# Packing the queries on GpSimd, with the loads, weights and bias rows around it laid out anew, in a hybrid decoder layer

## The chip, the cores and the metric

The kernel runs on one core of a Trainium2 chip. Its engines are TensorE (PE in the profile, with the weight loads as PEld), VectorE (DVE), ScalarE (ACT), GpSimd (POOL) and SyncE (SP). SP only issues transfers, ACT issues some too; an issue of ACT is shown as ACTq, one of SP as SPq. The metric is the device time of one execution in microseconds. Chances of "same" mean within 0.2% of the time before.

## The reference

The layer takes x (2048 tokens of 1024 channels, float32) and computes two mixers beside each other, an output projection and a squared-ReLU MLP:

```
n = RMSNorm(x)
gq, gk, gv, gr, glow, dq, dk, dv = split(n @ W_in)
o_a = GLA(gq, gk, gv, log_sigmoid(glow @ w2 + b) / 16)      # 4 heads, chunks of 64
o_a = RMSNorm per head(o_a) * g * silu(gr)
o_b = dilated attention(dq, dk, dv, rel_bias)                # 8 heads of 64
h = x + [o_a ; o_b] @ W_out
h = h + relu(RMSNorm(h) @ W_ff1)^2 @ W_ff2
y = RMSNorm(h)
```

GLA is linear attention with a forget gate, computed in chunks with a state of 64x128 per head that is carried from chunk to chunk. The dilated attention has three branches, with (window, dilation) of (128, 1), (512, 4) and (2048, 16). In a branch with dilation d the tokens are taken with stride d, and each query of a block of 128 sees the keys of its own block and the one before it, up to 128 steps back; a bias is added by bucket of distance. The three outputs are summed with weights proportional to their softmax denominators.

## The kernel before

All products are made in float32 or in a rounded format of it (fp32r). For the large ones each operand is split in two parts, high and low, and `mm3` (lines 66 to 69) sums three matmuls into a PSUM bank: high by high, low by high, high by low. The large products are done in seven block products in place of eight, so most stages run over seven jobs j in the order 1, 2, 5, 6, 3, 4, 7 and add or subtract blocks in between.

There are four stages. Up to about 589 us the **projections** run: 18 groups (nine groups of W_in's columns for two halves of the tokens), each of seven jobs, 126 jobs in all. `load_w` (line 181) loads pieces of the weights on SP's queue. `prep` (187) splits the weights of a job, on ACT (line 197) and DVE (199, 201), into one of three buffers `combs` (176), two jobs ahead of the product; on POOL it also forms the block sums that the next jobs need. `product` (270) multiplies. Six groups are narrow (two times 128 columns: the queries and keys of both mixers); there the weights are held in the array and 512 tokens are moved, so that the result is transposed. Three are wide (two times 256, or 264); there the tokens are held and the weights moved. A buffer of `combs` is laid out for pieces of 264 columns in any case, so the pieces of 128 or 256 columns stand 1,056 bytes apart. `finish` (230) stores the results in DRAM, for most groups on ACT's queue.

During the second half, `bias_rows` (320) makes for each branch and head a row of 384 biases and stores it (`rowD`), and `spread_bias` (333) copies each row 128 times within DRAM (`rbD`), so that a later load can read it with each partition shifted by one. It is called three times, six jobs apart, once for each branch; each is one transfer of 1,536 KB on SP's queue.

Next is the **mixer** (about 589 to 993 us). The dilated attention is cut into 160 units, 20 for each of eight heads: 4 for the branch with dilation 16 (`br` 2), and 8 each for `br` 1 and `br` 0. A unit computes scores on PE (lines 624, 626), adds the bias and takes the row minimum on DVE (636), exponentiates on ACT (637), transposes on PE (646), copies the transposed probabilities out of PSUM on ACT or DVE in turn (653, 655), multiplies with the values on PE (665) and copies the result on DVE (668). Step k of the main loop interleaves the scores of unit k+3, the transposes of unit k and the values of unit k-2.

For the branches 2 and 1 the queries of a block are not neighbours. `pack_q` (567) copies a head's queries into a buffer `qp` where they are, in four parts of 128x512 for each of the two branches, so 64 copies in all, on ACT (line 578). The main loop calls them four to one units ahead of the branch's first unit. `load_head` (518) loads a head's queries (`qs`, each half of the partitions in its own transfer) and its keys in two parts (`k1`, `k2`, each twice): six transfers of 512 KB, thirteen units ahead. After two heads `combine` (684) loads stored results of two branches, computes the weights on DVE (699 to 710) and sums on POOL (716, 718), for the last two heads on DVE.

The GLA part, called the gated part here, runs in the same loop: `gla_steps` (798) is a generator of 79 short steps, five for each block of 128 tokens. It has PE products, exponentials and squares on ACT (784, 785, 818, 820), products on POOL (786, 787, 833, 834) and the state's update on DVE (844, 847). The loop takes a step of it from unit G0 on, GE times in 100 units: with 16 and 65, the steps end near unit 138.

At the start of the mixer, the loads are written in this order (862 to 867): the first head's queries and keys, the values of the three branches, the biases of the three branches (eight loads each; POOL reorders those of branches 1 and 0, lines 559 and 562), then the gated part's buffers, constants and first blocks.

Last come the **output projection** (to about 1228 us) and the **MLP**, which the change doesn't touch.

What sets the order of the work: only the first part of the projections has its order written out by hand. Elsewhere a planner goes through the program with estimated durations and puts, on each engine and each queue, the operation next that is ready and stands first in the program; an operation written later can so come earlier. An engine or a queue then runs in the order planned, and waits where its next operation isn't ready. Large tiles share 25 slots of 8,448 bytes in each partition, so a load also waits until a slot is free.

Of the kernel before, what the change touches and what calls it, by code (L numbers as in the profile page):

```python
# [10 lines left out]
F32 = mybir.dt.float32  # L11
FR = mybir.dt.float32r
I32 = mybir.dt.int32
AF = mybir.ActivationFunctionType
# [19 lines left out]
XSC = {0: (3,), 1: (4,), 2: (5,), 3: (), 4: (6,)}  # L34
TOP = (5,)
OTHER = [7, 9, 10, 11, 12] + [14 * k + n for k in (1, 2, 3) for n in (0, 4, 7, 8, 9)]
G0, GE = 16, 65
RELOAD = (10, 11, 12)
BANKS = {"a": 2, "c": 3, "d": 2, "o": 1}

# [1 line left out]
def emit(tc, a, stop=99):  # L42
# [15 lines left out]
    def view(t, shape):  # L58
        n = int(np.prod(shape))
        names = "abcd"[:len(shape)]  # L60
        return t[:, :n].rearrange(f"p ({' '.join(names)}) -> p {' '.join(names)}", **dict(zip(names, shape)))
# [111 lines left out]
    jobs = [(g, j) for g in range(2 * NG) for j in order]  # L173
    w_in = a["w_in"].rearrange("o (c p) n -> p (o c) n", p=128)
    raws = [view(slot("wraw"), (2, 4, 264)) for _ in range(2)]
    combs = [view(slot("wcomb", FR), (2, 4, 264)) for _ in range(3)]
    TF = {j: [slot(f"tb{j}", FR) for _ in range(2)] for j in order}
    TB = {j: [view(t, (4, 512)) for t in TF[j]] for j in order}
    nTD = dram.tile([7, 128, 4, 512], F32, name="nTD")
# [1 line left out]
    def load_w(g, n, k):  # L181

        if g < 2 * NG:
            _, c0, w = groups[g % NG]
            SP.dma_start(raws[n][:, k, :, :w], w_in[:, 4 * k:4 * k + 4, c0 + n * w:c0 + n * w + w])

    def prep(at):

        if at >= len(jobs):
            return  # L190
        g, j = jobs[at]
        kind, _, w = groups[g % NG]
        (a11, a12), (a21, a22) = [[raws[n][:, k, :, :w] for k in range(2)] for n in range(2)]
        hi, lo = combs[at % 3][:, 0, :, :w], combs[at % 3][:, 1, :, :w]
        src = {1: a11, 2: a12, 5: a21, 6: a21, 3: a12, 4: a22, 7: a21}[j]
        sc = scales.get(kind, 1.0)
        A.activation(hi, src, AF.Copy, scale=sc)  # L197
        if sc == 1.0:
            V.tensor_tensor(lo, src, hi.bitcast(F32), op=OP.subtract)  # L199
        else:  # L200
            V.scalar_tensor_tensor(lo, src, sc, hi.bitcast(F32), op0=OP.mult, op1=OP.subtract)
        if j == 2:
            G.tensor_tensor(a21, a21, a22, op=OP.add)
        if j == 5:
            G.tensor_tensor(a21, a21, a11, op=OP.subtract)
            load_w(g + 1, 0, 0)
            G.tensor_tensor(a12, a12, a21, op=OP.subtract)
        if j == 6:
            G.tensor_tensor(a21, a22, a21, op=OP.subtract)
        if j == 3:  # L210
            load_w(g + 1, 0, 1)
        if j == 4:
            load_w(g + 1, 1, 1)
        if j == 7:
            load_w(g + 1, 1, 0)
# [54 lines left out]
    def product(at, i):  # L270

        g, j = jobs[at]
        kind, _, w = groups[g % NG]
        p = ps("acao"[banks[0] % 4])
        banks[0] += 1
        B, W = TB[j], [combs[at % 3][:, q, :, :w] for q in range(2)]
        n = w
        if w == 128:
            n = 512
            for c in range(4):  # L280
                mm3(p, W[0][:, c], W[1][:, c], B[0][:, c], B[1][:, c], c == 0, c == 3)
        else:
            p = p[:, :w]
            tk = slice(i * 128, i * 128 + 128)
            for c in range(4):
                mm3(p, B[0][:, c, tk], B[1][:, c, tk], W[0][:, c], W[1][:, c], c == 0, c == 3)

        def rest():
            X, c11, c12, c21, c22 = [v[:, i * n:i * n + n] for v in (CX, *C[0], *C[1])]
            q = p  # L290
            if kind == "dq":
                q, ix, i11, i12, i21, i22 = [v.rearrange(f"p (c {o}) -> p c r i", c=4, i=8) for v, o in
                                             ((p, "r i"), *((v, "i r") for v in (X, c11, c12, c21, c22)))]
            else:
                ix, i11, i12, i21, i22 = X, c11, c12, c21, c22
            if j == 1:
                A.activation(ix, q, AF.Copy)  # L297
            elif j == 2:
                V.tensor_tensor(i11, q, ix, op=OP.add)
                finish(g, 0, 0, i)  # L300
            elif j == 5:
                A.activation(i22, q, AF.Copy)
            elif j == 6:
                V.tensor_tensor(ix, q, ix, op=OP.add)
                G.tensor_tensor(c12, X, c22, op=OP.add)
            elif j == 3:
                V.tensor_tensor(i12, q, i12, op=OP.add)
                finish(g, 0, 1, i)
            elif j == 4:
                A.activation(i21, q, AF.Copy)  # L310
            else:
                V.tensor_tensor(ix, q, ix, op=OP.add)
                G.tensor_tensor(c21, c21, X, op=OP.add)
                V.tensor_tensor(c22, c22, X, op=OP.add)
                finish(g, 1, 0, i)
                finish(g, 1, 1, i)

        return rest
# [11 lines left out]
            V.tensor_copy(rbo[:, d], p[:8, :384])  # L330
        SP.dma_start(rowD, rbo)

    def spread_bias(d):

        row = rowD[:, d]
        SP.dma_start(rbD[d].rearrange("h p n -> p h n"),
                     bass.AP(tensor=row.tensor, offset=row.offset, ap=[[0, 128], [3 * 384, 8], [1, 384]]))

    def split(hi, lo, src):
        A.activation(hi, src, AF.Copy)  # L340
# [154 lines left out]
    for at in range(5, len(jobs)):  # L495
        g = jobs[at][0]
        if at + 2 > 6:
            prep(at + 2)
        if at in (7 * NG - 9, 7 * NG - 8):
            back.append(reload(order[at - 7 * NG + 9]))  # L500
        for i in range(4 if groups[g % NG][2] > 128 else 1):
            product(at, i)()
        if g == NG - 1:
            back.pop(0)()
            if at + 2 < 7 * NG:
                back.append(reload(order[at + 2 - 7 * NG + 7]))
        if at in OTHER:
            next(other)
        if at == 7 * NG + 2:
            bias_rows()  # L510
        if at in (7 * NG + 8, 7 * NG + 14, 7 * NG + 20):
            spread_bias((at - 7 * NG - 8) // 6)
    if stop <= 1:
        es.close()
        return
# [2 lines left out]
    def load_head(h):  # L518
        pr, hh = divmod(h, 2)
        qs, k1, k2 = slot("qs", FR, S), slot("k1", FR, S), slot("k2", FR, S)  # L520
        rows = slice(64 * hh, 64 * hh + 64)
        for dup in range(2):
            half = slice(64 * dup, 64 * dup + 64)
            SP.dma_start(qs[half].bitcast(F32), qD[pr][dup, rows])
            SP.dma_start(k1[half].bitcast(F32), kD[pr][0, rows])
            SP.dma_start(k2[half].bitcast(F32), kD[pr][1, rows])
        return qs, k1, k2

    def load_v(pr, br):
# [37 lines left out]
    def pack_q(h, br, part):  # L567
# [7 lines left out]
        else:  # L575
            dst = dst.rearrange("e (r i) -> e r i", r=16)[:, 4 * part:4 * part + 4]
            src = src.rearrange("e (i r) -> e r i", r=16)[:, 4 * part:4 * part + 4]
        A.activation(dst, src.bitcast(F32), AF.Copy)

    def windows(br, n):  # L580

# [279 lines left out]

    pairs, outs = {0: load_head(0)}, {}
    ring["pes"], ring["pts"] = view(slot("pe"), (4, 512)), view(slot("pt"), (4, 512))
    vs = {(0, br): load_v(0, br) for br in (2, 1, 0)}
    for d in (2, 1, 0):
        load_bias(d)
    gla_start()
    WOAT = {(7, 2): 3, (7, 1): 2, (6, 0): 2, (7, 0): 1}

    def alternate(*streams):  # L870
# [229 lines left out]
    for at, t in enumerate(tiles):  # L1100
# [3 lines left out]
        h = u[:, 1]  # L1104
# [258 lines left out]
```

## Time and profile before

| | us |
|---|---|
| median of 3 runs | 2445.02 (2440.99 to 2446.39) |
| the profiled execution | 2445.35 |
| its span, first to last instruction | 2443.6 |
| PE busy, of the span | 2331.5 |
| DVE, ACT, POOL busy | 1585.7, 1196.0, 488.6 |
| mean granted clock of PE | 0.982 |

A line of the profile's groups or of the timeline names the line of the program, the engine and the operation, then the tile written, an arrow, and the tiles read, with the shape. In a timeline the first two numbers are the start and the duration in us; several operations of one kind in a row are merged, as x6; in brackets stand the idle time of the engine before and what ended it. Matmuls overlap in the pipeline: one shows 0.39 us, but the next starts about 0.23 us later, so steps are read from the starts. The granted clock is 1.00 most of the time and 0.50 in some stretches of 3.4 or 6.8 us, mostly after PE was idle.

### The profile page before, as it was taken

The page shows a single profiled execution, that of the slowest core. Times are in us where ns is not written, and L with a number is a line of the kernel's source. Part 1 is how long each engine was busy: PE and PEld are TensorE (multiplying, and loading weights), DVE is VectorE, ACT ScalarE, POOL GpSimd, SP SyncE. Part 2 cuts the span into 40 slices and gives each one's busy share as a digit, 9 for nine tenths or more (in the row PEclk, how much of TensorE's full clock was granted, in tenths as well). Part 3 has the DMA queues.
Part 4 walks back from the last instruction along what each step waited for, and adds up shares of the span by engine and source line. Part 5 has one row for each costly group of instructions (what it writes and reads, how often), then busy time and mean ns, then how long its engine had stood idle before and what let it go on. Part 6 is the DMA issues. An engine that isn't in the chain of part 4 may idle for free.

```text
span 2443.6 us, 34989 instructions
## 1 busy us (share of the span) xinstructions
PE 2331.5 (95%) x12648; PEld 1998.8 (82%) x12648; DVE 1585.7 (65%) x2971; ACT 1196.0 (49%) x2215; POOL 488.6 (20%) x425
## 2 busy tenths in 40 slices
PE   6999997999889989999999999999999999999998
PEld 6877887778889888888878887888888888888887
DVE  6877666764567768644677778877774354555554
ACT  5565434534767768323455556655553232234323
POOL 5555435444044534000000000000000000001002
PEclk8999998999999989999999999999999999999999
DMA  6457763747677875567754446644458576556653
GB/s 156 122 157 233 231 197 99 213 147 198 161 186 213 208 197 172 172 215 233 254 195 158 142 147 207 213 168 145 143 194 289 167 276 210 185 189 231 224 165 103
DMA packets 343514, 459.16 MB, mean 188 GB/s; under 512 B 19572, under 2 KB 216453, under 8 KB 337070
## 3 DMA queue, kind: packets, MB, share of 16 engines
q1 hardware_dynamic: 317854, 418.92, 55.8%
q10 hardware_dynamic: 25488, 38.02, 4.4%
q8 instruction: 99, 1.62, 0.3%
q14 instruction: 73, 0.60, 0.1%
HBM read 294.03 MB, written 167.55 MB: 189 GB/s over the span
## 4 chain that ended last, share of the span: by engine, by line
PE 74%; DMA 8%; DVE 7%; ACT 5%; issue 3%; POOL 2%; ACTq 0%; SPq 0%; POOLq 0%; DVEq 0%
PE ps_a L67 8%; PE ps_a L69 8%; PE ps_a L68 8%; PE ps_c L67 7%; PE ps_c L69 7%; PE ps_c L68 7%; PE ps_d L67 4%; PE ps_d L69 4%; PE ps_d L68 4%; PE ps_a L665 3%; PE ps_o L67 3%; PE ps_o L69 3%; PE ps_o L68 3%; PE ps_d L646 2%; DMA wraw<-w_in 2%
## 5 line engine op out<-in xcount | busy, mean ns | idle before, releaser
L1197 POOL TENSOR_TENSOR suma<-suma,gs 128x512 f32<-128x512 f32 x16 | 23.3, 1472 | 1153.2 <-ACT scr L1195 1153.1
L341 DVE TENSOR_TENSOR ca<-ra,ca 128x1024 fp32r<-128x1024 f32 x112 | 137.8, 1230 | 163.1 <-ACT ca L340 163.1
L340 ACT ACTIVATE ca<-ra 128x1024 fp32r<-128x1024 f32 x112 | 118.0, 1053 | 224.9 <-PE ps_c L69 184.5
L340 ACT ACTIVATE w1comb<-w1raw 128x512 fp32r<-128x512 f32 x224 | 139.5, 627 | 159.6 <-PE ps_c L69 56.6
L665 PE MATMUL ps_a<-v,pt 128*128 128x65 f32 x1200 | 181.1, 263 | 13.0 <-ACT pt L653 10.3
L665 PEld LDWEIGHTS ps_a<-v,pt 128*128 128x128 f32 x1200 | 174.5, 199 | 18.6 <-ACT pt L653 12.0
L341 DVE TENSOR_TENSOR w1comb<-w1raw,w1comb 128x512 fp32r<-128x512 f32 x224 | 153.8, 689 | 53.9 <-ACT w1comb L340 53.6
L637 ACT ACTIVATE pe<-pe,O 128x256 f32<-128x256 f32 (+1 forms) x384 | 155.3, 455 | 59.6 <-DVE O L636 54.9
L646 PE MATMUL ps_d<-ident,pe 128*128 128x128 f32 x600 | 149.6, 285 | 8.6 <-DVE gla L796 6.8
L636 DVE CUSTOM_DVE_ANT_0 pe<-ps_c,nb 128x256 f32<-128x256 f32 (+1 forms) x384 | 126.7, 360 | 45.2 <-PE ps_d L646 25.5
L197 ACT ACTIVATE wcomb<-wraw 128x512 fp32r<-128x512 f32 (+2 forms) x126 | 96.4, 774 | 98.7 <-PE ps_a L69 23.3
L199 DVE TENSOR_TENSOR wcomb<-wraw,wcomb 128x512 fp32r<-128x512 f32 (+2 forms) x84 | 99.3, 1187 | 58.7 <-ACT wcomb L197 56.0
L340 ACT ACTIVATE cb<-rb 128x1024 fp32r<-128x1024 f32 x56 | 59.4, 1060 | 159.2 <-PE ps_o L68 105.8
L67 PE MATMUL ps_c<-hb,w1comb 128*128 128x512 f32 x336 | 131.6, 392 | 4.3 <-ACT hb L340 4.3
L68 PE MATMUL ps_c<-hb,w1comb 128*128 128x512 f32 x336 | 131.5, 391 | 1.6 <-DVE w1comb L341 1.6
L69 PE MATMUL ps_c<-hb,w1comb 128*128 128x512 f32 x336 | 131.1, 390 | 0.0
L67 PE MATMUL ps_c<-cb,ca 128*128 128x512 f32 x336 | 130.7, 389 | 0.0
L68 PE MATMUL ps_c<-cb,ca 128*128 128x512 f32 x336 | 130.7, 389 | 0.0
L69 PE MATMUL ps_c<-cb,ca 128*128 128x512 f32 x336 | 130.7, 389 | 0.0
L67 PE MATMUL ps_a<-wcomb,tb 128*128 128x256 f32 (+1 forms) x336 | 99.1, 295 | 19.2 <-ACT acc L297 12.5
L646 PEld LDWEIGHTS ps_d<-ident,pe 128*128 128x128 f32 x600 | 105.5, 184 | 11.1 <-DVE gla L796 7.3
L1063 ACT ACTIVATE acc<-acc 128x512 f32<-128x512 f32 x128 | 79.7, 631 | 56.3 <-DVE acc L1083 35.8
(352 smaller groups left out, 7247.1 us busy)
## 6 DMA issues: line engine op xcount, KB each, us to landing
ra<-actD SPq DMA_DIRECT2D x56, 1024.0 KB, 6.2
actD<-acc SPq DMA_DIRECT2D x192, 256.0 KB, 2.4
rb<-w_ff SPq DMA_DIRECT2D x72, 512.0 KB, 4.6
w1raw<-w_ff SPq DMA_DIRECT2D x32, 1024.0 KB, 5.6
k<-kD SPq DMA_DIRECT2D x32, 512.0 KB, 10.4
rb<-hTD SPq DMA_DIRECT2D x14, 1024.0 KB, 5.6
wraw<-w_in SPq DMA_DIRECT2D x48, 256.0 KB, 3.5
boD<-O SPq DMA_DIRECT2D x8, 1056.0 KB, 5.5
```

The lines of the kernel that those rows point to most:

```text
L67: T.matmul(out, sh, mh, start=first, stop=False)
L68: T.matmul(out, sl, mh, start=False, stop=False)
L69: T.matmul(out, sh, ml, start=False, stop=last)
L197: A.activation(hi, src, AF.Copy, scale=sc)
L199: V.tensor_tensor(lo, src, hi.bitcast(F32), op=OP.subtract)
L340: A.activation(hi, src, AF.Copy)
L341: V.tensor_tensor(lo, src, hi.bitcast(F32), op=OP.subtract)
L636: V.tensor_tensor_reduce(p, s, bias, scale=1.0, scalar=BIG, op0=OP.add, op1=OP.min, accum_out=nm)
L637: A.activation(p, p, AF.Exp, bias=nm, scale=-1.0)
L646: T.transpose(pb[:, i * 128:i * 128 + 128], src, ident)
L665: T.matmul(self.b.opsum[:, n % 4], self.pt[:, i * 128:i * 128 + 128], self.b.v[:, blk, cols], start=first, stop=last)
L1063: A.activation(v, v, AF.Relu)
```

## The change

There are six edits.

- `pack_q` copies on POOL instead of ACT.
- The gated part starts at unit 8 instead of 16 and takes 56 steps in 100 units instead of 65.
- `load_head` loads both halves of the queries first, then both halves of the first part of the keys, then of the second.
- The weights' buffers of the projections are laid out by the width of the group: pieces of 128 or 256 columns now stand 1,024 bytes apart, those of 264 columns 1,056 bytes as before. A new function `comb` gives the two parts for `prep` and `product`.
- `spread_bias` copies the rows of two heads of one branch at a time, on ACT's queue, so twelve transfers of 384 KB take the place of three of 1,536 KB. They are written three jobs apart, over jobs 72 to 105, from branch 2 to branch 0; before, branch 0 came first.
- At the start of the mixer the loads are written by branch, bias before values, and the gated part's loads come after those of branch 2.

```diff
-G0, GE = 16, 65
+G0, GE = 8, 56
...
-    combs = [view(slot("wcomb", FR), (2, 4, 264)) for _ in range(3)]
+    combs = [slot("wcomb", FR) for _ in range(3)]
...
+    def comb(at, w):
+
+        t = view(combs[at % 3], (2, 4, max(w, 256)))
+        return [t[:, q, :, :w] for q in range(2)]
...
-        hi, lo = combs[at % 3][:, 0, :, :w], combs[at % 3][:, 1, :, :w]
+        hi, lo = comb(at, w)
...
-        B, W = TB[j], [combs[at % 3][:, q, :, :w] for q in range(2)]
+        B, W = TB[j], comb(at, w)
...
-    def spread_bias(d):
+    def spread_bias(d, h):
 
-        row = rowD[:, d]
-        SP.dma_start(rbD[d].rearrange("h p n -> p h n"),
-                     bass.AP(tensor=row.tensor, offset=row.offset, ap=[[0, 128], [3 * 384, 8], [1, 384]]))
+        row = rowD[h:, d]
+        A.dma_start(rbD[d][h:h + 2].rearrange("h p n -> p h n"),
+                    bass.AP(tensor=row.tensor, offset=row.offset, ap=[[0, 128], [3 * 384, 2], [1, 384]]))
...
-        if at in (7 * NG + 8, 7 * NG + 14, 7 * NG + 20):
-            spread_bias((at - 7 * NG - 8) // 6)
+        if 7 * NG + 8 <= at < 7 * NG + 44 and at % 3 == 0:
+            spread_bias(2 - (at - 7 * NG - 8) // 12, (at - 7 * NG - 8) // 3 % 4 * 2)
...
-        for dup in range(2):
-            half = slice(64 * dup, 64 * dup + 64)
+        halves = [slice(64 * dup, 64 * dup + 64) for dup in range(2)]
+        for dup, half in enumerate(halves):
             SP.dma_start(qs[half].bitcast(F32), qD[pr][dup, rows])
-            SP.dma_start(k1[half].bitcast(F32), kD[pr][0, rows])
-            SP.dma_start(k2[half].bitcast(F32), kD[pr][1, rows])
+        for part, t in enumerate((k1, k2)):
+            for half in halves:
+                SP.dma_start(t[half].bitcast(F32), kD[pr][part, rows])
...
-        A.activation(dst, src.bitcast(F32), AF.Copy)
+        G.tensor_copy(dst, src)
...
-    vs = {(0, br): load_v(0, br) for br in (2, 1, 0)}
+    vs = {}
     for d in (2, 1, 0):
         load_bias(d)
-    gla_start()
+        vs[0, d] = load_v(0, d)
+        if d == 2:
+            gla_start()
```

## The prediction

> **What bounds the kernel now.** I read the page's first part, then the busy time of each engine by stage, then what PE's idle times ended on, and last the timelines of the other engines around those. The page says that PE is the bound:
>
> ```profile
> PE 2331.5 (95%) x12648; PEld 1998.8 (82%) x12648; DVE 1585.7 (65%) x2971; ACT 1196.0 (49%) x2215; POOL 488.6 (20%) x425
> ```
>
> By stage (columns: stretch, length, then PE, PEld, DVE, ACT, POOL busy, granted clock, DMA share, GB/s) PE is never idle in the feed-forward part, which the change doesn't touch, and idle for 12, 15 and 14 us in three stretches of the mixer:
>
> ```profile
> 585.00:640.00 55.00, 43.23 (x340) 41.43 (x340) 28.95 (x131) 40.15 (x77) 13.08 (x20) 0.88 0.84 200
> 640.00:900.00 260.00, 245.41 (x2002) 233.87 (x2001) 178.91 (x744) 188.65 (x488) 101.53 (x107) 0.97 0.78 199
> 900.00:1010.00 110.00, 96.26 (x771) 89.81 (x771) 91.54 (x357) 71.91 (x176) 40.02 (x37) 0.95 0.59 178
> 1540.00:2000.00 460.00, 460.00 (x2032) 380.88 (x2030) 300.99 (x415) 222.66 (x345) 6.04 (x4) 1.00 0.57 194
> ```
>
> So a gain can come from PE's idle times before 1010 us, from the half clock after them, or from a shorter step of PE. The timeline of PE shows the three large idle times in the mixer (in brackets: idle before, and what ended it):
>
> ```profile
> 626.54 2.39 PE L665 MATMUL ps_a<-v,pt 128*128 128x65 f32 x10 [5.54 <-ACT pt L653]
> ...
> 724.32 0.58 PE L624 MATMUL ps_c<-k,qs 128*128 128x256 f32 x1 [6.32 <-DVE O L636]
> ...
> 905.00 1.11 PE L646 MATMUL ps_d<-ident,pe 128*128 128x128 f32 x4 [6.39 <-DVE gla L796]
> ```
>
> The first is ACT's. Its queue holds packs in bursts, and exponentials and copies of probabilities stand behind them:
>
> ```profile
> 617.87 5.86 ACT L578 ACTIVATE qp<-qs 128x512 fp32r<-128x512 f32 x6 [2.31 <-DMA qs<-qD]
> 623.54 0.46 ACT L637 ACTIVATE pe<-pe,O 128x256 f32<-128x256 f32 x1
> 623.91 1.93 ACT L578 ACTIVATE qp<-qs 128x512 fp32r<-128x512 f32 x2
> ```
>
> The second and third are DVE's: it stands in its queue before the combine's first operation, whose loads are late, although ACT has a burst at 715.24 too:
>
> ```profile
> 723.75 0.17 DVE L699 TENSOR_TENSOR small<-O,cmb 128x16 f32<-128x16 f32 x1 [8.27 <-DMA cmb<-boD]
> ...
> 902.09 0.17 DVE L699 TENSOR_TENSOR small<-O,cmb 128x16 f32<-128x16 f32 x1 [8.76 <-DMA cmb<-boD]
> ```
>
> Before the mixer the one large idle time is PE's 11.4 us up to 380.95, ended by ACT's L297. ACT's own timeline shows why it came late: stores of the projections stand in its queue and are let go one by one.
>
> ```profile
> 359.48 0.53 ACTq L266 DMA_DIRECT2D vN<-acc  x1
> 359.75 1.08 ACT L197 ACTIVATE wcomb<-wraw 128x1056 fp32r<-128x1056 f32 x1
> 367.56 0.53 ACTq L266 DMA_DIRECT2D vN<-acc  x1
> 372.24 0.33 ACTq L264 DMA_DIRECT2D vD<-acc  x1
> 373.87 0.53 ACTq L266 DMA_DIRECT2D vN<-acc  x1
> ```
>
> The three transfers that spread the bias rows were issued by SP at 349.79 to 351.2 and land after 17.1 us in the median, and the weight load issued at 354.12 landed 19.7 us later, at 373.85. The stores move on just when these land (their data had been ready since 365.5). So slow transfers on SP's queue held ACT.
>
> Last, PE's steps. In the projections with the weights held, and in the feed-forward products of the same shape:
>
> ```profile
> 519.55 0.39 PE L69 MATMUL ps_c<-tb,wcomb 128*128 128x512 f32 x1
> ...
> 522.12 0.39 PE L69 MATMUL ps_a<-tb,wcomb 128*128 128x512 f32 x1
> ```
>
> ```profile
> 1299.39 0.39 PE L67 MATMUL ps_a<-hb,w1comb 128*128 128x512 f32 x1
> ...
> 1302.11 0.39 PE L67 MATMUL ps_c<-hb,w1comb 128*128 128x512 f32 x1
> ```
>
> These are 11 steps in 2.57 us, 0.2336 each, and 12 in 2.72, 0.2267 each, at a granted clock of 1.00 both times.
>
> **The change part by part.** The sum is made against the profiled execution: 2445.35 us, of which 2443.6 are the span and 1.75 lie around it. The median of the runs shown is 2445.02, so nothing has to be shifted.
>
> *Weights at multiples of 1 KB.* Pieces of the weights stood 1,056 bytes apart; the feed-forward pieces stand 512 bytes apart. If that is the difference, the 1,008 matmuls of 512 columns in the six narrow groups save 0.0069 us each, 7.0 us, in stretches where PE is busy throughout (20.00 of 20 from 540 to 560). The 1,344 of 256 columns step by 0.118 (from 339.77 to 342.01, 19 steps); half of 0.2267 would save up to 6 us more, but the mixer's score products, whose operands stand at multiples of 512 bytes, show 0.12 as well, so I take nothing there. The 672 of 264 columns keep their spacing. Ends: 13 us gained, or nothing, if something else in the projections makes the step long; a loss is left out, because every row at such spacings has the short step. I take -7.
>
> *Bias rows in twelve pieces on ACT's queue.* What can go is the 11.4 us, and about 2.5 us in which PE ran at half clock afterwards (380.95 to about 386): 14 us. What comes are twelve issues on ACT, by SP's rows 0.62 us each, 7.4 us, past exponentials and weight copies. They are written three jobs apart, but the planner issued the three of before back to back, though they are written six jobs apart; so I expect the twelve bunched soon after the row table lands at 349.8. Then ACT loses some 7 us while PE still has products with prepared weights, and the stores wait again, though for transfers a quarter as large and not behind the weight load. Ends: -14 (spread out, all hidden) and +6 (ACT's 7.4 us on PE's path, the old wait kept). I take -7, halfway to the full gain, because the weight load no longer stands behind 4.7 MB in its own queue.
>
> *Start of the mixer.* PE waits 2.39 us for the gated part's loads, 2.08 for the first pack, 1.33 for an exponential, and loses 1.5 at half clock: 7.3 us. The gated loads now come ahead of sixteen bias loads, so the 2.39 should go; ACT begins its exponentials without the eight packs it ran from 593.31 to 601. But the packs are now behind POOL's copies of the bias (0.61 to 0.64 us for 256 columns), which end at 598.97; the first pack at the end of these would set the first score back from 594.4 to about 600. Values and bias loads only swap places on SP: 42 issues to the same end. Ends -7 and +6, and I take 0.
>
> *Packs on POOL.* ACT loses 64 packs of 1.09 us, 70 us in all. On PE's path were 5.54, then 1.30 and 1.07 at 825 and 829, 1.76 at 856, with half clock after the first (2.5 us lost) and after the last (3.4): 15.6 us. POOL gains 64 copies of 512 columns; by the bias copies, 1.25 us each, 80 us, in a stretch where it is busy 155 of 425 us. This is hidden as long as a head's packs are done before its first score. Head 1's queries landed at 617.9 and its packs are needed some 20 us later; eight take 10 us. Behind a pack that waits for its queries stand the gated part's products and the combine's, which PE and DVE wait for in turn. Queries loaded ahead of keys bring their second half forward by two of six loads; the keys' end is the same. Ends: -15.6, and +5 if the gated part is held as the exponentials were. I take -10, about two thirds, because the burst at 618 is alone in being plainly what ended the wait.
>
> *The combine's late loads* (6.32 and 6.39, with 1.5 at half clock after each) are not touched. The planner orders SP anew, so between -16 and +8; I take 0.
>
> *Gated part from unit 8.* Its 79 steps end at unit 150 in place of 138, of 160. That moves seven of them, 1.4 blocks of about 4 us on PE, into the last stretch, where PE had 3.9 us idle between 960 and 1000, but DVE was busy 33 of 40. Ends -4 and +5; I take 0.
>
> Sum: -7 - 7 + 0 - 10 + 0 + 0 = -24, so 2445.35 - 24 = 2421 us.
>
> **The rivals.**
>
> *Packs late on POOL (slower).* POOL works in order, and its operations often wait: L833 up to 21.7 us for ACT, L716 up to 4.7 for DVE. A pack behind such a wait makes PE wait at the first score of a head. One such wait costs what the one at 724 does, 6.3 and 1.5, some 8 us. There are seven changes of head. With the packs' gain lost and -14 from the first two terms, two late heads (16) decide for slower; four give 2445 - 14 + 32 = 2463. For it: that ACT's packs did just this. Against it: 20 us of lead, and POOL idle from 607.5 to 635.4.
>
> *Bias issues bunched on ACT.* +6 in place of -7: 2434.
>
> *Little happens.* The short step isn't due to the spacing, and PE's idle times only move to the next late load: 2445, give or take 5. For it: half of the large idle times are the combine's loads.
>
> *DVE held by POOL.* L847, with both inputs in SBUF, takes 0.42 us in the median but up to 2.31, and 19.9 us in 30 where 12.6 would do: 7.3 us lost, with POOL busy 155 us. With 235 us it would be 11.1, so 3.8 us more of DVE, all on the path at worst: 2425. The Trainium skill (SBUF — State Buffer, section SBUF: two separate sides) has this as a rule: GpSimd and VectorE share a pair of ports, held for a whole instruction, against VectorE operations with two SBUF inputs or in a two-port mode. By that rule the trace agrees in L847, and in the scores' L636 (one input from PSUM, 0.426 us at most), which stays free; the rule speaks against this move, but only for few operations.
>
> **How the numbers follow.** The forecast (2421) gets 0.52, the bunched issues (2434) 0.14, the held DVE (2425) 0.06, little happens 0.08, late packs 0.20. A change below 0.2%, 4.9 us, can't be told from none. Faster: 0.52 + 0.14 + 0.06 = 0.72; same 0.08; slower 0.20. The likeliest case alone spans 2400 to 2442 by its ends (they won't all fall together); the range reaches up into the late packs, to 2454.
>
> **What would show it.** Steps of 0.227 in the narrow projections; no 11 us of PE idle near 370, and where ACT issues the bias rows; no ACT burst at 618 and no PE wait after it; POOL's packs near 1.25 us, and ended before each head's first score. It is wrong if PE's waits end on packs, if L699 still waits 8 us more often than twice, or if the step stays at 0.2336.

## The result and the profile after

The changed kernel takes 2430.9 us in the median of 6 runs (2429.18 to 2433.72), the kernel before 2448.08 (2440.99 to 2452.97) on the same chip: a ratio of 0.9931, with a 95% interval from 0.9913 to 0.9949. That is 0.7% faster, 17.2 us by the medians. The forecast was 2421 us, the range 2400 to 2454. The profiled execution of the changed kernel took 2433.72 us (span 2431.9) against 2445.35 before, 11.6 us less: it is the longest of its six, so the traces show only these 11.6 of the 17.2 us. Most lines of the changed program stand 5, 6 or 8 further down: ACT's weight copy L197 is now L202, the stores' copy L310 is L315, `pack_q`'s copy L578 is L584, and the combine's first operation L699 is L705.

The page's first part, of the changed kernel:

```profile
PE 2327.0 (96%) x12648; PEld 1999.9 (82%) x12648; DVE 1595.3 (66%) x2971; ACT 1142.5 (47%) x2151; POOL 550.3 (23%) x489
```

ACT lost 53 us and POOL gained 62, where the prediction had 70 and 80: the packs have moved. PE still bounds the kernel. The stretches of the mixer and of the MLP, in the columns of before (stretch, length, busy PE, PEld, DVE, ACT, POOL, granted clock, DMA share, GB/s):

```profile
585.00:640.00 55.00, 48.96 (x406) 47.34 (x405) 33.80 (x158) 31.64 (x86) 32.09 (x40) 0.94 0.95 221
640.00:900.00 260.00, 242.20 (x2020) 232.62 (x2019) 187.41 (x778) 158.48 (x450) 146.42 (x153) 0.96 0.79 205
900.00:1010.00 110.00, 97.17 (x720) 89.27 (x720) 90.15 (x316) 58.81 (x146) 38.75 (x34) 0.94 0.50 160
1540.00:2000.00 460.00, 460.00 (x2032) 380.96 (x2031) 298.26 (x404) 219.78 (x336) 6.04 (x4) 1.00 0.58 196
```

In the first stretch PE is busy 5.7 us longer and issues 66 matmuls more: the burst of packs on ACT near 618 is gone. The MLP is as it was. From the starts of PE's instructions, the 11.6 us come from these parts: the projections' last product starts 2.2 us earlier (588.5 to 586.3), the first score comes 1.1 us later after it (6.0 to 7.0), from the first score to the first transpose of the output projection go 13.1 us less (398.9 to 385.8), the output projection takes 4.4 more, the first half of the MLP 1.8 less. The largest idle times of PE in the mixer, in its timeline:

```profile
593.34 0.58 PE L630 MATMUL ps_c<-k,qp 128*128 128x256 f32 x1 [5.52 <-POOL qp L584]
...
707.66 0.77 PE L819 MATMUL ps_o<-gla 128*128 128x256 f32 x1 [5.09 <-DVE gla L853]
...
888.22 0.47 PE L671 MATMUL ps_a<-v,pt 128*128 128x65 f32 x1 [7.91 <-DVE pt L661]
```

The wait of 5.54 us behind ACT's burst has no successor. At the start PE waits for the first pack, on POOL; near 707 for a DVE operation of the gated part; near 888 still for DVE, which stood before the third combine:

```profile
887.39 0.17 DVE L705 TENSOR_TENSOR small<-O,cmb 128x16 f32<-128x16 f32 x1 [9.81 <-DMA cmb<-boD]
```

The start in POOL's timeline: the packs stand behind a copy of the bias that waited for its load, the bound that the prediction had named.

```profile
591.65 0.60 POOL L565 COPY nb<-nb 128x256 f32<-128x256 f32 x1 [3.56 <-DMA nb<-rbD]
592.20 0.14 POOL L538 MEMSET v<- 128x32 f32 x1
592.26 7.95 POOL L584 CAST qp<-qs 128x512 fp32r<-128x512 f32 x8
```

In the projections the twelve transfers of bias rows are in ACT's timeline, eight of them within 6 us, and below them PE's idle times that stand in the place of the 11.39 us up to 380.95:

```profile
351.63 1.92 ACTq L341 DMA_DIRECT2D rbD<-rowD  x3
...
357.05 0.60 ACTq L341 DMA_DIRECT2D rbD<-rowD  x1
...
362.45 3.54 ACTq L341 DMA_DIRECT2D rbD<-rowD  x2
...
380.13 1.08 ACT L202 ACTIVATE wcomb<-wraw 128x1056 fp32r<-128x1056 f32 x1 [9.37 <-DMA vN<-acc]
```

```profile
369.78 0.58 PE L67 MATMUL ps_o<-wcomb,tb 128*128 128x256 f32 x1 [5.28 <-ACT acc L315]
...
381.27 0.39 PE L67 MATMUL ps_c<-wcomb,tb 128*128 128x264 f32 x1 [1.46 <-ACT wcomb L202]
```

So 6.7 us of idle time in place of 11.4. The narrow groups' steps, in PE's timeline of the changed kernel:

```profile
520.89 0.39 PE L67 MATMUL ps_o<-tb,wcomb 128*128 128x512 f32 x1
...
523.61 0.39 PE L67 MATMUL ps_a<-tb,wcomb 128*128 128x512 f32 x1
```

These are 12 steps in 2.72 us, 0.2267 each, the MLP's step, where 0.2336 was in the prediction's row. That row of before was a long one: over all undisturbed steps of the narrow groups the median is 0.232 before and 0.227 after. The groups of 256 columns went the other way. First before, then after, 30 steps each:

```profile
558.07 0.28 PE L67 MATMUL ps_a<-wcomb,tb 128*128 128x256 f32 x1
...
561.62 0.28 PE L67 MATMUL ps_c<-wcomb,tb 128*128 128x256 f32 x1
```

```profile
558.00 0.28 PE L67 MATMUL ps_a<-wcomb,tb 128*128 128x256 f32 x1
...
561.59 0.28 PE L67 MATMUL ps_a<-wcomb,tb 128*128 128x256 f32 x1
```

3.55 us against 3.59; over all 1,344 the median step is 0.118 before and 0.120 after, 2 to 2.7 us in all.

Single executions also differ by PE's clock. The trace records stretches with a granted clock of 0.50, mostly 3.4 or 6.8 us long (before, one of 13.7 us from 372.3 on). Half of PE's busy time in them is counted here as lost; this is an estimate from the clock records of each trace. In the projections from 60 us on, the changed kernel loses 11.2 us so, where 7.4 were lost before. Without these the projections got 6.0 us shorter, not 2.2, and PE's idle time there fell from 35.6 to 30.1 us. In the mixer the loss is 12.9 us before and 12.8 after, in the output projection 1.7 and 3.4.

### The profile page after: what moved, and what is told of

Same layout as the page of the kernel before. It is cut to its first block, busy times and chain, and to the rows that moved or that the text cites. A ratio compares the mean times of both kernels' runs of the same rounds, so it can differ in the third digit from the quotient of the medians.

```text
span 2431.9 us, 35003 instructions
## 1 busy us (share of the span) xinstructions
PE 2327.0 (96%) x12648; PEld 1999.9 (82%) x12648; DVE 1595.3 (66%) x2971; ACT 1142.5 (47%) x2151; POOL 550.3 (23%) x489
## 4 chain that ended last, share of the span: by engine, by line
PE 79%; DVE 7%; DMA 7%; ACT 2%; issue 2%; POOL 1%; SPq 0%; ACTq 0%; POOLq 0%; DVEq 0%
PE ps_a L67 8%; PE ps_a L68 8%; PE ps_a L69 8%; PE ps_c L67 7%; PE ps_c L69 7%; PE ps_c L68 7%; PE ps_d L67 4%; PE ps_d L69 4%; PE ps_d L68 4%; PE ps_a L671 4%; PE ps_o L67 3%; PE ps_o L68 3%; PE ps_o L69 3%; PE ps_d L652 2%; PE ps_c L630 2%
## 5 line engine op out<-in xcount | busy, mean ns | idle before, releaser
L671 PEld LDWEIGHTS ps_a<-v,pt 128*128 128x128 f32 x1200 | 172.6, 198 | 12.5 <-DVE pt L661 10.9
L202 ACT ACTIVATE wcomb<-wraw 128x512 fp32r<-128x512 f32 (+2 forms) x126 | 96.4, 774 | 108.2 <-PE ps_a L69 24.4
L94 POOL TENSOR_TENSOR stats<-stats,mhalf 128x1 f32<-128x1 f32 (+1 forms) x64 | 46.1, 725 | 299.6 <-DVE stats L93 255.0
L346 DVE TENSOR_TENSOR cb<-rb,cb 128x1024 fp32r<-128x1024 f32 x56 | 68.2, 1222 | 61.0 <-ACT cb L345 60.9
```

Source lines behind the costliest of these rows:

```text
L671: T.matmul(self.b.opsum[:, n % 4], self.pt[:, i * 128:i * 128 + 128], self.b.v[:, blk, cols], start=first, stop=last)
```

## The experiments

The prediction added up terms, one for each edit. So the first runs make each edit alone, and the next undo one edit of the changed kernel at a time. If the terms add up, the two series agree; if not, edits depend on each other. The table has each run's ratio to the kernel before with its interval, and from its profiled execution: the end of the projections, the time from there to the first transpose of the output projection (the mixer), and at the third combine DVE's wait for the loads, with PE's largest idle time there behind it (us). The two reorderings of loads count as one edit, so there are five.

| kernel | ratio [95%] | proj. end | mixer | DVE / PE |
|---|---|---|---|---|
| before | 1 | 588.5 | 404.8 | 8.8 / 6.4 |
| changed | 0.9931 [0.9913, 0.9949] | 586.3 | 392.8 | 9.8 / 7.9 |
| packs alone | 1.0022 [1.001, 1.0033] | 589.7 | 406.7 | 14.9 / 12.2 |
| weights alone | 1.0006 [0.9994, 1.0018] | 586.5 | 404.5 | 10.1 / 7.7 |
| bias rows alone | 0.9995 [0.9983, 1.0007] | 581.7 | 405.1 | 11.6 / 9.3 |
| gated part alone | 1.0062 [1.0044, 1.0081] | 586.3 | 407.8 | 14.7 / 12.2 |
| order of loads alone | 1.0004 [0.9996, 1.0012] | 588.4 | 406.5 | 10.9 / 8.5 |
| changed, packs undone | 1.0009 [0.9996, 1.0022] | 584.8 | 409.3 | 14.1 / 11.5 |
| changed, gated part undone | 0.9971 [0.9961, 0.9982] | 578.4 | 403.9 | 14.0 / 11.3 |
| changed, order undone | 0.9934 [0.9921, 0.9946] | 586.3 | 394.7 | 9.5 / 7.6 |
| changed, bias rows undone | 0.9952 [0.9934, 0.9969] | 587.4 | 392.7 | 9.7 / 7.8 |
| packs and gated part alone | 0.9982 [0.9972, 0.9991] | 588.9 | 394.6 | 8.6 / 6.7 |
| changed, stores on ACT | 0.9921 [0.9902, 0.994] | 580.1 | 387.8 | 6.8 / 5.4 |
| changed, combine later | 0.993 [0.9909, 0.995] | 576.1 | 387.8 | 7.6 / 5.7 |

The profiled executions of the gated part alone and of the changed kernel without it were 7 to 8 us shorter than their medians (2448.70 against 2456.58, 2431.56 against 2438.51), and that of the last kernel in the table 6.5 us (2420.18 against 2426.69), so their verdict is the ratio, and the trace only tells where they wait. The kernels were measured on different chips, each against the kernel before on its own chip. The end of the projections varies: 578.4 to 586.3 in the four kernels with both edits of the projections as in the changed one. Most of that is the clock: by the estimate above they take 515.0 to 516.7 us from 60 us on without the loss. The five kernels with neither edit take 517.0 to 521.1, the two with the weights' edit but not the bias rows' 519.7 and 520.2, the one with the bias rows alone 514.0.

**Packs alone.**

```diff
-        A.activation(dst, src.bitcast(F32), AF.Copy)
+        G.tensor_copy(dst, src)
```

> Only the packs go to GpSimd; all else is the kernel before. Theory A (ACT's bursts of packs made the mixer long): ACT loses about 64 x 1.09 us, the mixer (first score to first transpose of the output projection, 399 us before, 386 us in the changed kernel) becomes about 10 us shorter, no idle time of PE near 620 ends on ACT's copy of probabilities, and the time is 10 us (0.4%) less. Theory B (the planner's other order of loads or the gated part's spread gave the mixer's gain): the mixer stays within 4 us of 399, and the time within 5 us.

Measured: 0.2% slower. The stall behind ACT's burst is gone, as predicted: from the first value product of head 0 to that of head 1 go 38.4 us in place of 47.6. But the first score is at 602.0 in place of 594.4, and the last three stages from head to head are 5.9, 2.1 and 5.3 us longer. The third combine in DVE's timeline, and PE's behind it:

```profile
903.72 0.17 DVE L699 TENSOR_TENSOR small<-O,cmb 128x16 f32<-128x16 f32 x1 [14.86 <-DMA cmb<-boD]
```

```profile
904.31 0.48 PE L646 MATMUL ps_d<-ident,pe 128*128 128x128 f32 x1 [12.16 <-DVE gla L796]
```

So neither theory held as put: the mixer from the first score on is 4.5 us shorter (394.4), not 10, and the time is longer. The packs' gain is real where it was predicted, and lost at the start and around the combines.

**Weights alone.**

```diff
-    combs = [view(slot("wcomb", FR), (2, 4, 264)) for _ in range(3)]
+    combs = [slot("wcomb", FR) for _ in range(3)]
...
+        t = view(combs[at % 3], (2, 4, max(w, 256)))
+        return [t[:, q, :, :w] for q in range(2)]
...
```

> Only the spacing of the weights in the projections' buffers; the planner's order stays the same. Theory A (the spacing sets PE's step): the step of the narrow groups goes from 0.233 to 0.227 us (1,008 matmuls, -6 us) and that of the groups of 256 columns from 0.118 to 0.120 (1,344, +2.6 us); with PE the bound the projections end about 3.5 us sooner. Theory B (another edit, such as the bias rows' transfers, changed the steps): steps of 0.233 and 0.118 as before, and no change. Theory C (steps change, but the waits for ACT and DVE in the narrow groups take it back): projections end within 1.5 us of before.

Measured: no difference in the time. Here every engine has its instructions in the order of before, so the steps can only differ by the spacing: 0.227 in the narrow groups and 0.120 at 256 columns, just as in the changed kernel. The projections end 2.0 us earlier, between theories A and C.

**Bias rows alone.**

```diff
-        SP.dma_start(rbD[d].rearrange("h p n -> p h n"),
-                     bass.AP(tensor=row.tensor, offset=row.offset, ap=[[0, 128], [3 * 384, 8], [1, 384]]))
+        A.dma_start(rbD[d][h:h + 2].rearrange("h p n -> p h n"),
+                    bass.AP(tensor=row.tensor, offset=row.offset, ap=[[0, 128], [3 * 384, 2], [1, 384]]))
...
```

> Only the bias rows: twelve transfers on ACT's queue in place of three on SP's. Theory A: ACT issues most of the twelve between 350 and 363 us, PE's idle time before the wide group of 264 columns goes from 11.4 to about 5 us, and that group gets 4 to 5 us shorter; the time is 4 us less, if nothing in the mixer is reordered. Theory B (the weight load behind the spread rows on SP's queue was the whole wait): the idle time goes altogether, -11 us. Theory C: the wait only moves to ACT's own issues, no change within 2 us.

Measured: no difference in the time, although the projections end 6.8 us earlier. In place of the 11.39 us PE waits 3.57 (up to 363.22) and 3.97 (up to 376.00). The mixer is as long as before, and the output projection takes 216.8 us in place of 211.7, which gives most of it back in this execution; 2.8 of these 5.2 us are half clock by the estimate above (4.5 us lost, 1.7 before).

**Gated part alone.**

```diff
-G0, GE = 16, 65
+G0, GE = 8, 56
```

> Only the gated part's start and spread. Theory A (its place matters little, PE's work is the same): the mixer stays within 4 us of 399 and the time within 5 us. Theory B (its spread gave the mixer's gain): the mixer is about 10 us shorter, as in the changed kernel, and the stretch of the last head, without the gated part before, gets 3 to 5 us longer.

Measured: 0.6% slower. PE's wait behind ACT's burst, near 623, is still there (4.99 us), and the third combine costs 12.2 us of PE:

```profile
902.96 0.17 DVE L699 TENSOR_TENSOR small<-O,cmb 128x16 f32<-128x16 f32 x1 [14.74 <-DMA cmb<-boD]
```

The four single edits together come to +0.85% where the whole change gives -0.69%. So two theories were left: the fifth edit, the order of the loads, carries the gain (A), or edits depend on each other (B).

**Order of loads alone.**

```diff
-            SP.dma_start(k1[half].bitcast(F32), kD[pr][0, rows])
-            SP.dma_start(k2[half].bitcast(F32), kD[pr][1, rows])
+        for part, t in enumerate((k1, k2)):
+            for half in halves:
+                SP.dma_start(t[half].bitcast(F32), kD[pr][part, rows])
...
-    vs = {(0, br): load_v(0, br) for br in (2, 1, 0)}
+    vs = {}
     for d in (2, 1, 0):
         load_bias(d)
-    gla_start()
+        vs[0, d] = load_v(0, d)
+        if d == 2:
+            gla_start()
```

> The kernel before with the two changes of order alone: both halves of a head's queries loaded ahead of its keys, and at the start of the mixer the bias loads, values and gated part's loads interleaved. Theory A (the order of the loads carries the gain): 0.985 to 0.993 of before, the first score at 593, and the combine's subtraction waits less than the 21 us in all that it waits before. Theory B (no edit carries it; packs on POOL pay only together with the new order or the earlier gated part): 0.998 to 1.002, and ACT's burst with the 5.5 us wait behind it still there near 625.

Measured: 1.0004, the burst on ACT still ends a wait of 3.2 us at 626.87. Theory A is out.

**Packs undone.** The changed kernel, but:

```diff
-        G.tensor_copy(dst, src)
+        A.activation(dst, src.bitcast(F32), AF.Copy)
```

> The changed kernel with the packs back on ACT. Theory A: 0.993 to 0.996 of before, since the order alone carries the gain. Theory B: 0.998 to 1.004, the whole gain lost, a PE wait of 5 us for an exponential during head 0, and the stage from head 0's to head 1's first value product back from 43 to 47 us.

Measured: the whole gain is lost (1.0009). The burst is back on ACT, eight packs from 611.84 to 619.90, with 3.23 us of PE waiting behind it at 620.61, and the stage from head 0's to head 1's first value product is back at 47.8 us; the third combine makes DVE wait 14.09 us.

**Gated part undone.** The changed kernel, but:

```diff
-G0, GE = 8, 56
+G0, GE = 16, 65
```

> The changed kernel with the gated part from unit 16 to 65 again. The gated part's edit alone made the kernel before 0.6% slower. Theory A (its cost adds to the rest): 0.985 to 0.990 of before, better than the changed kernel. Theory B (the earlier gated part is what lets the combine and the packs pass each other on POOL): 0.997 to 1.004, with DVE's waits for the combine's loads back from 19 to 28 us or more.

Measured: 0.9971, four tenths of a per cent lost, and again the long third wait:

```profile
886.78 0.18 DVE L705 TENSOR_TENSOR small<-O,cmb 128x16 f32<-128x16 f32 x1 [13.97 <-DMA cmb<-boD]
```

So the edit that alone cost 0.6% is worth 0.4% beside the packs, as theory B had it: DVE's waits for the combine's loads come to 32.9 us, where the changed kernel has 18.9.

**Order undone.** The changed kernel with both hunks of the order of loads the other way round:

```diff
-        for part, t in enumerate((k1, k2)):
-            for half in halves:
-                SP.dma_start(t[half].bitcast(F32), kD[pr][part, rows])
+            SP.dma_start(k1[half].bitcast(F32), kD[pr][0, rows])
+            SP.dma_start(k2[half].bitcast(F32), kD[pr][1, rows])
...
```

> The changed kernel with both orders of the loads undone (keys beside queries; values, then bias, then the gated part's loads). Theory A: 1.003 to 1.009 of before, as the other four edits added up from their single runs (0.2, 0.1, -0.1 and 0.6%). Theory B: 0.993 to 0.997, near the changed kernel, since packs and gated part help each other without it.

Measured: 0.9934. The order of the loads does nothing that can be measured in the whole time, alone or beside the rest. In the trace it does one thing: with the packs on POOL the first score comes 10.6 us after the projections without it, and 7.0 with it; later stages take that up.

**Packs and gated part alone.** The kernel before with the first and fourth diff above.

> The kernel before with two of the five edits alone: packs on POOL and the gated part from unit 8. Alone the one took 0.2% more and the other 0.6% more. Theory B (the two carry the gain together): 0.992 to 0.996 of before, and 384 to 390 us from the first score to the first transpose of the output projection (394.4 with the packs alone, 402.3 with the gated part alone). Rival (the projections' edits are needed too): 0.997 to 1.002. If the two only added up: 1.008 and some 398 us.

Measured: 0.9982. In the whole time this lies in the rival's range, not in theory B's: two edits bring only 0.2% of the 0.7%. In the mixer it is all that theory B expected: 384.1 us from the first score to the output projection's first transpose, where the packs alone had 394.4 and the gated part alone 402.3, and the third wait is short again:

```profile
892.04 0.17 DVE L699 TENSOR_TENSOR small<-O,cmb 128x16 f32<-128x16 f32 x1 [8.62 <-DMA cmb<-boD]
```

The column of the mixer settles it: with neither of the two edits 404.5 to 406.5 us (four kernels), with the packs alone 403.9 and 406.7, with the gated part alone 407.8 and 409.3, with both 392.7 to 394.7 (four kernels). One of them brings nothing, both some 12 us. Without the half clock, by the estimate above, it is 378.0 to 383.1 us in all six kernels that have both, and 388.0 to 392.2 in the eight others, so some 11 us.

What the whole still lacks beside the changed kernel, some 12 us by the ratios, is outside the mixer. The kernel with the order undone differs from this one by the two edits of the projections alone, and the intervals of the two (0.9934 and 0.9982) are apart. So beside packs and gated part these edits bring some 0.5%, where alone each brought nothing. The profiled executions show 7.0 us of it, of which 2.6 are in the projections and 5.9 in the output projection, less 1.5 in the MLP; 1.7 of the 5.9 are half clock. The rest was not found.

**Bias rows undone.** The changed kernel, but:

```diff
-        A.dma_start(rbD[d][h:h + 2].rearrange("h p n -> p h n"),
...
+        SP.dma_start(rbD[d].rearrange("h p n -> p h n"),
...
```

> The changed kernel with the bias rows in three transfers on SP's queue again. Theory (once the mixer is right, the time saved in the projections is kept): PE's idle time of 10 to 11 us near 370 is back in place of 5.3 and 1.5, and the whole is 0.995 to 0.998 of before, 5 to 9 us above the changed kernel. Rival (as with the bias rows alone, which saved 6.8 us up to the end of the projections and nothing in the end): the later stages take it up and the whole stays at 0.992 to 0.994; the weights' spacing would then have to carry what parts the run with packs and gated part alone (0.9982) from the changed kernel (0.9931).

Measured: 0.9952, 0.2% or some 5 us above the changed kernel, though the two intervals overlap, so the loss isn't clear of noise. No run undoes the weights in the changed kernel. The wait is back:

```profile
381.14 0.59 PE L67 MATMUL ps_a<-wcomb,tb 128*128 128x264 f32 x1 [11.12 <-ACT acc L302]
```

**Stores on ACT's queue, and the spacing of 256 columns back.**

```diff
-    def issue_later(n, *args):
+    def issue_later(n, *args, q=SP):
...
-                        O.rearrange("p (b r) n -> p b (r n)", b=4))
+                        O.rearrange("p (b r) n -> p b (r n)", b=4), q=A)
...
-        t = view(combs[at % 3], (2, 4, max(w, 256)))
+        t = view(combs[at % 3], (2, 4, 256 if w == 128 else 264))
...
```

> The changed kernel with two edits: the 256-column groups' weight pieces back at 264 columns' spacing (the narrow groups keep the new one), and the stores of the branch outputs that the combine reads back issued by ACT in place of SP. For the first: steps of 0.227 in the narrow groups and 0.118 in the 256-column ones, the projections 2 to 3 us shorter. For the second, theory: the third combine waits because its store lands late behind the value loads of the next pair on SP's queue (12 to 15 us where a free one takes 5); on ACT's queue it lands in 4 to 6, from the store's issue to the combine's subtraction go 10 to 13 us in place of 17, DVE waits under 5 us in place of 9.8, PE under 4 in place of 7.9, and the whole gives 0.987 to 0.991 of before. Rival: the time lies in the loads that read it back, or the issues hold ACT: 0.992 to 0.996.

Measured: the steps are 0.227 and 0.118, as expected. The store's theory came half true. First the changed kernel in SP's timeline, then this one in ACT's and SP's:

```profile
870.23 0.53 SPq L740 DMA_DIRECT2D boD<-O  x1
...
875.27 4.05 SPq L698 DMA_DIRECT2D cmb<-boD  x2
```

```profile
856.60 0.40 ACTq L740 DMA_DIRECT2D boD<-O  x1
...
862.93 1.77 SPq L698 DMA_DIRECT2D cmb<-boD  x2
```

In the changed kernel the store lands 8.7 us after its issue, at 878.90. The second of the two loads waits for that and is issued at 878.96; its data are there 8.4 us later. On ACT's queue the store lands after 6.0 us, at 862.57, but the load that ends DVE's wait is issued 1.8 us after that and takes 10.6:

```profile
875.01 0.18 DVE L705 TENSOR_TENSOR small<-O,cmb 128x16 f32<-128x16 f32 x1 [6.79 <-DMA cmb<-boD]
```

From the store to DVE go 18.4 us, no less than the 17.2 of the changed kernel: what the store gained, the loads lost. DVE's wait is 3 us shorter because it arrives later. Before the change it was the store that was late, 12.4 us (885.49 to 897.85), and the first load behind it took 4.2; with the packs alone it was 15.4 and 4.2. Both parts move data while the DMA engines are busy, as the DMA share of the changed kernel shows, in stretches around its third combine (columns as above; the share is the last but one):

```profile
870.00:876.00 6.00, 6.00 (x50) 5.72 (x50) 3.94 (x19) 2.62 (x7) 0.55 (x1) 1.00 0.96 256
876.00:882.00 6.00, 4.31 (x40) 4.10 (x39) 1.55 (x10) 1.94 (x6) 3.46 (x6) 1.00 1.10 270
882.00:888.00 6.00, 0.00 (x0) 0.00 (x0) 0.61 (x2) 0.00 (x0) 1.86 (x2) 0.71 1.12 312
```

The 16 DMA engines are full while DVE waits. In SP's timeline two transfers of keys, the store and the gated part's loads are issued from 869.66 to 875, just ahead of the combine's. That this is why store and loads take so long is argued from these rows; no run took those transfers away.

**Combine later**, with the same spacing as in the run before.

```diff
-                        for n in (0, 2, 3, 4, 5, 6, 7):
+                        for n in (0, 4, 5, 6, 7, 8, 9):
```

> The changed kernel with the 256-column groups' spacing back as in the run on the stores, and the combine's operations written two units (some 5 us) later behind their loads. Theory (DVE's wait is the time from store to data, 16 to 20 us, less the lead that the order gives it, 2 to 8 us): the lead grows by about 5 us, the third combine's wait falls from 9.8 to 4 to 6 us, PE's from 7.9 to 2 to 4, 0.988 to 0.991 of before. Rival: another operation in DVE's order takes the wait over, or the later combine holds its buffers and the next loads: 0.992 to 0.997.

Measured: 0.993, the changed kernel's time. DVE comes to the combine 8.8 us after the store in place of 7.4, not 5 later: the planner places the operations by its own estimate, and writing them later moved them by 1.4 us. Neither of the last two runs can be told from the changed kernel by its time; the first has the lowest ratio of all, 0.9921. Their mixers of 387.8 us, 5.0 shorter than the changed kernel's, are in part the clock: 9.7 and 9.8 us are lost at half clock there, by the estimate above, in place of 12.8.

## Why the prediction was right, point by point

Its sign and its range were right, and 17 us of the 24 came. But the sum was right for another reason than its terms, so part of it is luck. By stages, the projections were forecast at -14 and gave -2.2 in the profiled execution (-6.0 without the half clock); the mixer was forecast at -10 and gave -12.0; the rest, forecast at 0, gave +2.5.

- **Weights, -7.** The mechanism was right: in the narrow groups the step fell by the spacing alone. Its size was not. The 0.0069 us a step came from one row of 11 steps, longer than most; by the medians it is 0.005, so 5 us for 1,008 steps. The step that failed is "a loss is left out, because every row at such spacings has the short step": at 256 columns the step grew by 0.002 in the median, 1,344 times, and took 2 to 2.7 us back. By the steps the term is some -2.4. Alone it ended the projections 2.0 us earlier, and no run shows it by itself in the whole time.
- **Bias rows, -7.** The twelve issues did bunch, as expected. The idle time fell by 4.7 us, and undoing the edit cost some 5, not clear of noise. Alone, what it saved up to the projections' end was given back later.
- **Start of the mixer, 0.** The first score came 7.0 us after the projections in place of 6.0, behind POOL's copies of the bias: the mechanism named, and nearly its net size. It hangs on the new order of the loads: 10.6 us without it, with the other edits kept.
- **Packs, -10, and gated part, 0.** This is the step that failed, as it was put: each edit a term of its own. The mixer gained 12.0 us, but neither edit makes that alone; the packs alone cost 0.2%, the gated part alone 0.6%, and the two together gain 0.2% of the whole. The packs' own cover held: 64 copies of 1.085 us in the mean, 64.6 us with overlaps counted once, against the 80 estimated, and PE waits for a pack at the first head alone.
- **The combine's loads, 0.** In the changed kernel that was right, 9.8 us where 8.8 were. What the prediction didn't see is that every edit of the mixer changes this wait by changing the planner's order. DVE's wait there is the time from the store to the data, less the time by which DVE comes later than the store. The first is 16 to 20 us in all these runs (16.6 before, 17.2 after, 19.6 with the packs alone, 16.4 with the gated part alone). The second is 7.8 us before and 7.4 after, but 4.7 with the packs alone and 1.6 with the gated part alone. Why the order comes out well with both and badly with either was not found: the planner orders by its estimated times, and no run changed those.
- **DVE held by POOL (a rival at 0.06).** The hold came, but that its size fits is luck. L853, which was L847, took 23.8 us in 30, where 19.9 were; 3.9 more, and 3.8 were worked out from POOL's busy time. But the whole excess lies in one instruction, and it is what PE's wait of 5.09 us up to 707.66 ends on. This line's two instructions in that stretch of the changed kernel (shortest, median and longest in ns, then first and last start), and POOL's timeline there:

```profile
L853 DVE TENSOR_TENSOR gla<-gla x2: 1012/3523/6034, 700.4 to 706.5; 64x256 f32<-64x256 f32 x2
```

```profile
699.71 1.03 POOL L840 TENSOR_TENSOR gla<-gla,stats 128x512 f32<-128x512 f32 x1
700.69 3.04 POOL L584 CAST qp<-qs 128x512 fp32r<-128x512 f32 x3
703.69 0.68 POOL L792 TENSOR_TENSOR gla<-gla 128x256 f32<-128x256 f32 x1
704.32 4.13 POOL L584 CAST qp<-qs 128x512 fp32r<-128x512 f32 x4
```

An operation of 0.42 us in the median lasted 6.03 (700.43 to 706.46), while POOL ran packs and products without a gap. It was there again without the bias edit (6.00) and with the combine later (6.03). With the packs on POOL in five other kernels the longest was 3.44 (stores on ACT), 3.17 (gated part undone), 3.10 (packs alone), 1.33 (packs and gated part) and 1.32 (order undone); with the packs back on ACT it was 1.45. In three of these five the line's sum is 18.3 to 19.6 us, below the 19.9 of before, so moving the packs to POOL did not by itself raise it. Nor is it shown to cost time: with the order undone the long hold is missing and the time is the same (0.9934); there PE waits 5.40 us up to 708.84, just behind the combine's subtraction, for whose loads DVE had waited 7.06.

The Trainium skill (SBUF — State Buffer, section SBUF: two separate sides) has the shared pair of ports locked for a whole instruction of the one or the other. The trace agrees that it is held, but for some six instructions of POOL in a row, not one. What let it go at 706.46, while POOL's packs ran on to 708.45, was not found.

- **Packs late on POOL, bunched issues on ACT, little happens.** The first is seen only with the first head, where PE waits 5.52 us for a pack. The second was half right: the issues bunched, and yet the idle time fell; what part they have in the 6.7 us left, no run shows. The third is what each edit alone gave, or worse: 0.9995 to 1.0062.

## What to carry to other kernels

Where a planner orders the work, the gains of edits need not add, and here they didn't: make each edit alone and undo each from the whole, and read the wait that the whole order sets (here DVE's, in front of loads that read back a store) in every run before crediting an edit. Here, with the DMA share at about 1, a store on another queue landed sooner (6.0 us in place of 8.7), and the time from the store to the data was no shorter (18.4 us against 17.2). An engine with room, such as POOL here, can still hold up another one's operation while its own follow each other without a gap. And before the stages of two single executions are compared, see how much of each ran at half clock.

## What the runs showed of the hardware that was not expected

- The spacing of the weight pieces moves the matmul's step both ways: 1,056 to 1,024 bytes takes it from 0.232 to 0.227 us in the median where the weights are held and 512 tokens moved, and from 0.118 to 0.120 where the weights are moved, 256 columns at a time. Back at 1,056 for the second kind alone, it is 0.118 again, with 0.227 kept in the first.
- A DVE operation with both inputs in SBUF was held for 6 us over several POOL operations that followed each other without a gap, in three kernels at the same place; in other kernels with the same copies on POOL the longest was 1.32 to 3.44 us.
